# Two more feed-forward pairs as seven block products, with two weight sums of each pair added by transfers

## The chip, the core and the metric

The kernel runs on one core of a Trainium2 chip. A core has TensorE (matmul, "PE" in the profile; its loading of the stationary operand is "PEld"), VectorE ("DVE"), ScalarE ("ACT"), GpSimd ("POOL") and SyncE ("SP", which only issues transfers here), a memory of 128 partitions that all of them share, PSUM banks into which TensorE accumulates, and 16 DMA engines. Each engine works through its own instructions in the order in which the program was built, and waits for others by semaphores. The metric is the device time of one execution in microseconds, and less is better.

## The reference

One layer of a decoder trunk on 256 tokens of width 1024: RMSNorm, a convolution module beside sparse attention, an output projection, cross-attention into 256 memory tokens, and a SwiGLU feed-forward of inner width 2816, each added to the residual, then a last RMSNorm. The change touches the feed-forward alone:

```python
def swiglu(h, w_in, w_out):          # w_in (1024, 5632), w_out (2816, 1024)
    a, b = jnp.split(h @ w_in, 2, axis=-1)
    return (jax.nn.silu(a) * b) @ w_out
...
    h = rms_norm(x, norm_ffn_g[l])
    x = x + swiglu(h, ffn_in_w[l], ffn_out_w[l])
return rms_norm(x, final_norm_g)
```

Everything is float32.

## The kernel before, in words

**Numbers.** To keep float32 precision, a factor is split in two parts of TensorE's faster format: ScalarE copies it (the high part, a name that ends in h) and VectorE subtracts that from the original (the low part, l). `split` (L173 and L175) does this for a transferred tile, `part` (L284 and L285) for a computed one. A product then takes three matmuls: high by high, low by high, high by low (`three`, L1194).

**First product of the feed-forward.** The loop over 22 chunks f0 to f21 (L1162, L1164) multiplies the normalized input `fg`, which lies in the double buffer LL, with 128 gate and 128 value columns at a time. Each chunk comes in two loads of 512 KB through four buffers of tag "w", which SP fills in order as they come free. ScalarE and VectorE combine the halves, apply 1/rms (L1167), silu and the product, and `part` splits the chunk's result for the second product.

**Second product.** The 22 chunks form 11 pairs. A pair is a 256x256 left factor (2 token blocks by 2 chunks, a11 to a22) times a 256x1024 right factor (2 chunks by 2 column halves of 512, b11 to b22). Plainly that is eight block products of three 128x512 matmuls each, added into four accumulators (`four_products`). The pairs in the tuple `SEVEN` use seven block products instead, by sums of blocks: four sums of the left blocks (`factors`, L1094, VectorE and one `part` while the first product still runs), four sums of the right blocks (`side`, L1104, VectorE), and three accumulators of their own (m1, m5 to m7), which the end combines (L1229). Such a pair has 21 matmuls instead of 24.

**Where the weights come from.** A pair's right factor is two loads of 512 KB. For the first pair of `SEVEN`, pair 1, they come long before and are worked on in pieces between the chunks (`weights_ahead`). For the others `weights_of_seven` loads w0 and w1 into "w" buffers (L1110), makes the four sums in a tile `tr`, and splits three plain blocks and four sums: each other pair into the fixed tiles th and tl, the rest through the five-deep buffers of `split` (ft). Pairs outside `SEVEN` use `half` (L212). The right factors' seven parts feed `seven_products`.

**The end.** The accumulators are combined on VectorE (L1229, L1280), squared on ScalarE, multiplied with the gain `gf` (L1236, two of them on GpSimd), scaled and sent. x3 and junk, the last stage's tiles, take over the buffer LL.

**Order.** The code is traced once, and a scheduler sets the order of each engine's instructions at build time; on the chip that order is fixed. `behind` and `in_line` keep some of them behind others on their engine.

Of the kernel before, what the change touches and what calls it, by code (L numbers as in the profile page):

```python
# [96 lines left out]
def tile_hybrid_block(  # L97
# [984 lines left out]
    even_odd, sums_of, parts, shl45 = [], {}, {}, []  # L1082

    def factors(i, even, odd):

# [4 lines left out]
        raw = small(f"sr{i}", [P, 4, P], tag="vw", bufs=4)  # L1090
        a11, a21, a12, a22 = even[:, 0:P], even[:, P:S], odd[:, 0:P], odd[:, P:S]
        for to, a, b, op in ((0, a21, a22, ALU.add), (1, a11, a21, ALU.subtract), (2, raw[:, 0], a11, ALU.subtract),
                             (3, a12, raw[:, 2], ALU.subtract)):
            nc.vector.tensor_tensor(out=raw[:, to], in0=a, in1=b, op=op)  # L1094
# [3 lines left out]
    SIDES = ((0, (0, 1), (0, 0)), (1, (1, 0), (0, 1)), (2, (1, 0), 0), (3, (1, 1), 2))  # L1098

    def side(tr, w, n):  # L1100

# [2 lines left out]
        return nc.vector.tensor_tensor(out=tr[:, to], in0=pick(a), in1=pick(b), op=ALU.subtract)  # L1104

    def weights_of_seven(i):

        w0, w1 = w = [small(f"fo{i}_{n}", [P, 2, 512], tag="w", bufs=4) for n in range(2)]
        for n in range(2):
            nc.sync.dma_start(w[n], wfo[i, n])  # L1110
# [16 lines left out]
        return bs + ts

    def weights_ahead(i):

# [1 line left out]
        w = [both[:, 0:2], both[:, 2:4]]
        for n in range(2):
            nc.sync.dma_start(w[n], wfo[i, n])
# [3 lines left out]
        for n in range(4):  # L1138
            side(tr, w, n)
# [296 lines left out]
```

## Time and profile before

| | |
|---|---|
| median of 3 runs | 546.23 us (546.1 to 546.39) |
| the profiled execution's own time | 546.24 us |
| its span, first to last instruction | 544.5 us |
| granted TensorE clock, mean | 0.997 of full speed |
| first product, first and last chunk's matmuls | about 355 to 485.6 us |
| second product, to its last matmul | 464.9 (pair 1's first), then 475.9 to 538.3 us |
| busy in the span: PE, DVE, ACT, POOL | 536.9, 457.1, 356.5, 150.2 us |
| fo loads (second product's weights) | 22 of 512 KB, median 4.0 us from issue to landing |

A timeline row gives start, duration, engine, line, operation, output<-inputs, shape and, in brackets, how long the engine had been idle before and what ended it. Rows on SPq are the issue of a transfer, not the transfer. A row of a stretch table is named by its two times. Names are the program's with buffer numbers left out, so fo stands for the weights of every pair and also for the four accumulators. GpSimd issues no transfer in this kernel.

### The profile page before, as it was taken

The numbers are of one execution on the slowest core, as the hardware profiler recorded it, in microseconds if no ns is written. First come the engines' busy times: TensorE is split into PE (matmuls) and PEld (weight loads), VectorE is DVE, ScalarE is ACT, GpSimd is POOL, SyncE is SP. The second block draws the span as 40 slices with busy tenths as digits, with TensorE's granted clock in tenths as the row PEclk, the third lists the DMA queues.
The fourth block names the chain that finished last, engine by engine and source line by source line (L and its number), as shares of the span: only waits on it lengthen the run. The fifth ranks groups of instructions, "written<-read, shape, count | busy, mean of one in ns | idle before, by whom it ended". The sixth has DMA issues, their size and how long they took to land.

```text
span 544.5 us, 10498 instructions
## 1 busy us (share of the span) xinstructions
PE 536.9 (99%) x3970; PEld 502.7 (92%) x3970; DVE 457.1 (84%) x914; ACT 356.5 (65%) x642; POOL 150.2 (28%) x103
## 2 busy tenths in 40 slices
PE   9999999999999999999999999999999999999995
PEld 8999999999999998999999999988888888888874
DVE  3998999899889898975859676688899998898986
ACT  4676466678855978779447664556665676647553
POOL 0069999898990000300004000230000000000001
PEclk9999999999999999999999999999999999999998
DMA  8927955554424653334755643536455664535632
GB/s 303 406 89 260 360 162 188 198 178 155 155 99 147 205 172 114 119 117 156 227 189 173 225 156 99 175 117 222 162 183 198 194 201 154 184 126 169 217 119 78
DMA packets 29155, 97.32 MB, mean 179 GB/s; under 512 B 3120, under 2 KB 5680, under 8 KB 28848
## 3 DMA queue, kind: packets, MB, share of 16 engines
q1 hardware_dynamic: 28384, 95.42, 52.4%
q10 hardware_dynamic: 720, 1.23, 0.6%
q8 instruction: 31, 0.51, 0.4%
q14 instruction: 20, 0.16, 0.1%
HBM read 95.39 MB, written 1.25 MB: 177 GB/s over the span
## 4 chain that ended last, share of the span: by engine, by line
PE 61%; DVE 1%; issue 0%; DVEq 0%
PE ps_f L1162 15%; PE ps_f L1164 8%; PE fo L1194 7%; PE ps_pw L240 4%; PE ps_xq L240 4%; PE ps_wo L240 4%; PE ps_xo L240 4%; PE ps_v L240 4%; PE m L1194 3%; PE xo_ps L964 1%; PE xs L964 1%; PE o L795 1%; PE pt_a L774 1%; PE s L729 1%; PE o L792 1%; PE pt_b L774 0%
## 5 line engine op out<-in xcount | busy, mean ns | idle before, releaser
L416 DVE SCALAR_TENSOR_TENSOR yp<-vt,ppt,yp 128x256 f32<-128x256 f32 x196 | 78.5, 484 | 0.3
L1236 POOL TENSOR_TENSOR x<-y,gf 128x512 f32<-128x512 f32 x2 | 2.6, 1297 | 172.6 <-issue 172.6
L1162 PE MATMUL ps_f<-g,f_1h 128*128 128x512 f32 x176 | 49.1, 398 | 0.0
L1162 PE MATMUL ps_f<-g,f_0h 128*128 128x512 f32 x176 | 48.2, 396 | 0.0
L1162 PEld LDWEIGHTS ps_f<-g,f_1h 128*128 128x128 f32 x176 | 32.9, 188 | 7.5
L1162 PEld LDWEIGHTS ps_f<-g,f_0h 128*128 128x128 f32 x176 | 30.1, 188 | 4.0
L175 DVE TENSOR_TENSOR f_1l<-f,f_1h 128x1024 fp32r<-128x1024 f32 x22 | 27.5, 1249 | 5.7 <-ACT f_1h L173 4.1
L1164 PEld LDWEIGHTS ps_f<-g,f_0l 128*128 128x128 f32 x176 | 27.0, 189 | 3.9
L1164 PE MATMUL ps_f<-g,f_0l 128*128 128x256 f32 x176 | 28.3, 283 | 0.0
L175 DVE TENSOR_TENSOR f_0l<-f,f_0h 128x1024 fp32r<-128x1024 f32 x22 | 26.8, 1219 | 1.7 <-ACT f_0h L173 1.7
L173 ACT ACTIVATE f_1h<-f 128x1024 fp32r<-128x1024 f32 x22 | 23.3, 1057 | 7.5 <-PE ps_xo L240 3.7
L1164 PE MATMUL ps_f<-g,f_1l 128*128 128x256 f32 x176 | 26.5, 281 | 0.0
L175 POOL TENSOR_TENSOR u_0l<-u,u_0h 128x1024 fp32r<-128x1024 f32 x7 | 17.3, 2467 | 31.1 <-DVE kt L502 31.1
L173 ACT ACTIVATE f_0h<-f 128x1024 fp32r<-128x1024 f32 x22 | 23.1, 1050 | 1.3 <-PE ps_xo L240 1.3
L749 ACT ACTIVATE p<-p,mins 128x256 f32<-128x256 f32 x32 | 15.9, 501 | 11.7 <-DVE mins L734 11.7
L1165 ACT ACTIVATE ab<-ps_f 128x256 f32<-128x256 f32 x44 | 16.5, 375 | 10.5 <-PE ps_f L1164 10.3
L1164 PEld LDWEIGHTS ps_f<-g,f_1l 128*128 128x128 f32 x176 | 23.3, 188 | 0.0
L428 POOL TENSOR_TENSOR yt<-yt,vw 128x512 f32<-128x512 f32 x17 | 23.0, 1353 | 0.7 <-ACT vw L425 0.3
L1166 DVE TENSOR_TENSOR ab<-ps_f,ab 128x256 f32<-128x256 f32 x44 | 18.3, 419 | 3.4 <-ACT ab L1165 3.2
L1169 ACT ACTIVATE sl<-ab 128x256 f32<-128x256 f32 x22 | 9.2, 417 | 15.4 <-DVE ab L1167 14.9
L284 ACT ACTIVATE uh<-sl 128x256 fp32r<-128x256 f32 x22 | 9.1, 414 | 14.0 <-DVE sl L1170 13.9
L944 POOL COPY acc<-s_wo 128x256 f32<-128x256 f32 x1 | 0.7, 659 | 62.6 <-ACT s_wo L937 62.6
(629 smaller groups left out, 1711.9 us busy)
## 6 DMA issues: line engine op xcount, KB each, us to landing
f<-in_wst_dram SPq DMA_DIRECT2D x44, 512.0 KB, 5.7
fo<-in_wfo_dram SPq DMA_DIRECT2D x22, 512.0 KB, 4.0
u<-in_wst_dram SPq DMA_DIRECT2D x14, 512.0 KB, 7.7
q<-in_wst_dram SPq DMA_DIRECT2D x8, 512.0 KB, 5.1
ga<-in_wst_dram SPq DMA_DIRECT2D x8, 512.0 KB, 3.8
gc<-in_wst_dram SPq DMA_DIRECT2D x8, 512.0 KB, 3.8
v<-in_wst_dram SPq DMA_DIRECT2D x8, 512.0 KB, 6.6
pw<-in_wst_dram SPq DMA_DIRECT2D x8, 512.0 KB, 4.8
```

The costliest lines, as they stand in the source:

```text
L173: copy = nc.scalar.activation(hi, w, AF.Copy)
L175: splits[name] = copy, eng.tensor_tensor(out=lo, in0=w, in1=f(hi[:]), op=ALU.subtract)
L240: mm = nc.tensor.matmul(ps[:, b], lhsT=lhsT, rhs=rhs, start=row + b + kb == 0, stop=kb == NB - 1 and row == 2 and b == 1)
L416: nc.vector.scalar_tensor_tensor(out=out[:, i] if t == ts[-1] else acc[i], in0=v, scalar=w, in1=acc[i], op0=ALU.mult, op1=ALU.add)
L428: nc.gpsimd.tensor_tensor(out=yt[:, 0:2], in0=yt[:, 0:2], in1=pr, op=ALU.add)
L749: exp.append(nc.scalar.activation(p1[k][:, br], p1[k][:, br], AF.Exp, scale=-1.0, bias=mins[:, hd, 1, br:br + 1], accum_out=sums[:, hd, 1, ...
L964: mm = nc.tensor.matmul(o, lhsT=lhsT, rhs=rhs, start=n == 0, stop=n == len(order) - 1)
L1162: nc.tensor.matmul(ps, lhsT=hs[kb // 4][0][:, kb % 4, cs], rhs=fg[:, :, kb], start=kb == 0, stop=False)
L1164: nc.tensor.matmul(ps[:, 1], lhsT=hs[kb // 4][1][:, kb % 4, cs], rhs=fg[:, 0, kb], start=False, stop=kb == NB - 1)
L1165: nc.scalar.activation(ab[:, b], ps[:, 0], AF.Copy)
L1166: joins[b] = nc.vector.tensor_tensor(out=ab[:, b], in0=ps[:, 1], in1=ab[:, b], op=ALU.add)
L1194: mm = nc.tensor.matmul(o, lhsT=a[x], rhs=b[w], start=start and n == 0, stop=stop and n == 2)
```

## The change

`SEVEN` grows from pairs 1, 2, 4, 5, 7, 8 to pairs 1 to 8. Of the four sums of right blocks, two no longer run on VectorE. For these, `paired` loads two neighbouring blocks (512 KB) into a tile with a plain transfer from SP, and GpSimd then issues a second transfer of 512 KB, which reads the blocks shifted by one from HBM and adds them to the tile in place (`accum_op=ALU.add`). The host's order of the blocks and the signs of the sums are changed to suit (the sums are additions now, and some later additions are subtractions). VectorE makes the two remaining sums from these (`side`, L1116 now) in one half of a tile `spare`.

The plain blocks come in a load of 256 KB and one of 512 KB, so a pair moves 1.75 MB instead of 1 MB. The tiles for the transferred sums are: for pair 1 the tile `tr` of `weights_ahead`; for pair 2 a second half of `gf`; for pairs 3 to 6 the halves of junk and x3, which lie in LL; for pairs 7 and 8 the second half of gf and the first half of junk again. Two more sets of left sums need homes as well: spare places in uh2 and ul2, and buffers of tag p0.

```diff
-SEVEN = (1, 2, 4, 5, 7, 8)
+SEVEN = (1, 2, 3, 4, 5, 6, 7, 8)
...
+    homes, coming = [], []
+
+    def paired(i, t):
+
+        nc.sync.dma_start(t, wfo[i, :, 0:2])
+        nc.gpsimd.dma_start(t, wfo[i, :, 1:3], accum_op=ALU.add)
+        return t
+
+    def side(tb, ta, w, n):
+
+        return nc.vector.tensor_tensor(out=tb[:, n], in0=w[:, n], in1=(ta, tb)[n][:, 0], op=ALU.add)
+
+    def ahead_of(i):
+
+        n = SEVEN.index(i) - 1
+        if n == 1:
+            homes.extend(t[:, c] for t in (junk, x3) for c in range(2))
+        coming.append(paired(i, homes[n % 5]))
...
     def weights_of_seven(i):
-        w0, w1 = w = [small(f"fo{i}_{n}", [P, 2, 512], tag="w", bufs=4) for n in range(2)]
-        for n in range(2):
-            nc.sync.dma_start(w[n], wfo[i, n])
-        tr = long(f"tr{i}", 10, (P, 4, 512))
-        for n in range(4):
-            with behind(*joins[n // 2:n // 2 + 1] if i == SEVEN[1] else ()):
-                side(tr, w, n)
-        b0, b1 = split(w0[:, 0:1], [P, 1, 512], f"fo{i}_0"), split(w1, [P, 2, 512], f"fo{i}_1")
+        w0 = small(f"fo{i}_0", [P, 1, 512], tag="w", bufs=4)
+        w1 = small(f"fo{i}_1", [P, 2, 512], tag="w", bufs=4)
+        nc.sync.dma_start(w0, wfo[i, :, 0:1])
+        nc.sync.dma_start(w1, wfo[i, :, 2:4])
+        n = SEVEN.index(i)
+        ta, tb = coming[n - 1], spare[:, 2 * (n % 2):2 * (n % 2) + 2]
+        for nxt in SEVEN[len(coming) + 1:n + 3]:
+            ahead_of(nxt)
+        for k in range(2):
+            with behind(*joins[k:k + 1] if i == SEVEN[1] else ()):
+                side(tb, ta, w1, k)
+        b0, b1 = split(w0, [P, 1, 512], f"fo{i}_0"), split(w1, [P, 2, 512], f"fo{i}_1")
...
     def weights_ahead(i):
...
+        paired(i, tr[:, 0:2])
+        nc.sync.dma_start(both, wfo[i])
...
-    gf = long("gf", 11, (P, 2, 512))
-    nc.sync.dma_start(gf, gfo)
+    gf = long("gf", 11, (P, 4, 512))
+    nc.sync.dma_start(gf[:, 0:2], gfo)
+    homes.append(gf[:, 2:4])
...
+        if j == 12:
+            ahead_of(SEVEN[1])
...
+    spare = long("spare", 10, (P, 4, 512))
```

In the built programs the places that matter are these. The first is SP's queue in the second product (fo4_1 is the second load of pair 4; x3 stands for the tile that holds x3 and junk). Before:

```order
L1110 DMA fo2_0_6131<-in_wfo_dram 128x1024
L1110 DMA fo2_1_6132<-in_wfo_dram 128x1024
L212 DMA fo3_0_6177<-in_wfo_dram 128x1024
L212 DMA fo3_1_6195<-in_wfo_dram 128x1024
L1110 DMA fo4_0_6213<-in_wfo_dram 128x1024
L1110 DMA fo4_1_6214<-in_wfo_dram 128x1024
L1110 DMA fo5_0_6257<-in_wfo_dram 128x1024
```

And now:

```order
L1129 DMA fo2_0_6149<-in_wfo_dram 128x512
L1130 DMA fo2_1_6150<-in_wfo_dram 128x1024
L1129 DMA fo3_0_6196<-in_wfo_dram 128x512
L1130 DMA fo3_1_6197<-in_wfo_dram 128x1024
L1129 DMA fo4_0_6239<-in_wfo_dram 128x512
L1110 DMA x3_6085<-in_wfo_dram 128x1024 x4
L1110 DMA gf_4716<-in_wfo_dram 128x1024
L1130 DMA fo4_1_6240<-in_wfo_dram 128x1024
L1129 DMA fo5_0_6284<-in_wfo_dram 128x512
```

The plain loads of five sums stand between fo4_0 and fo4_1: pairs 3 to 6, whose home is LL, and pair 7. The first of the four waits for the last matmul on fg.

The second place is VectorE behind the last chunk (sl21 is that chunk's product; an l at the end of a name is a low part; L175 is a split, L1104 or L1116 a sum). Before:

```order
L175 TENSOR_TENSOR fo3_0l_6180<-fo3_0_6177,fo3_0h_6179 128x1024
L285 TENSOR_TENSOR ul2_4713<-sl21_6060,uh2_4710 128x256
L1104 TENSOR_TENSOR tr4_6217<-fo4_0_6213 128x512
L1104 TENSOR_TENSOR tr4_6217<-fo4_1_6214,fo4_0_6213 128x512
L175 TENSOR_TENSOR fo3_1l_6198<-fo3_1_6195,fo3_1h_6197 128x1024
L175 TENSOR_TENSOR fo4_0l_6223<-fo4_0_6213,fo4_0h_6222 128x512
L1104 TENSOR_TENSOR tr4_6217<-fo4_1_6214,tr4_6217 128x512
L175 TENSOR_TENSOR fo4_1l_6227<-fo4_1_6214,fo4_1h_6226 128x1024
```

And now:

```order
L175 TENSOR_TENSOR fo3_1l_6209<-fo3_1_6197,fo3_1h_6208 128x1024
L285 TENSOR_TENSOR ul2_4713<-sl21_6077,uh2_4710 128x256
L175 TENSOR_TENSOR fo4_0l_6248<-fo4_0_6239,fo4_0h_6247 128x512
L175 TENSOR_TENSOR fo4_1l_6252<-fo4_1_6240,fo4_1h_6251 128x1024
L1116 TENSOR_TENSOR spare_6084<-fo3_1_6197,x3_6085 128x512
L285 TENSOR_TENSOR tl3_6213<-x3_6085,th3_6212 128x1024
L1116 TENSOR_TENSOR spare_6084<-fo4_1_6240,x3_6085 128x512
L1116 TENSOR_TENSOR spare_6084<-fo3_1_6197,spare_6084 128x512
L175 TENSOR_TENSOR ft4_0l_6256<-x3_6085,ft4_0h_6255 128x1024
```

The split of fo4_1 now stands ahead of all sums of pairs 3 and 4, which need the transferred sums in x3's tile.

The third is GpSimd's queue around the sum of squares behind the cross-attention (acc_2, from which the feed-forward's 1/rms comes):

```order
L1111 DMA gf_4716<-in_wfo_dram 128x1024
L944 COPY acc_2_3990<-s2_xo0_4596 128x256
L946 TENSOR_TENSOR acc_2_3990<-acc_2_3990,s2_xo0_4596 128x256
L946 TENSOR_TENSOR acc_2_3990<-acc_2_3990,s2_xo1_4617 128x256 x2
L946 TENSOR_TENSOR acc_2_3990<-acc_2_3990,s2_xo2_4656 128x256 x2
L946 TENSOR_TENSOR acc_2_3990<-acc_2_3990,s2_xo3_4695 128x256 x2
L1111 DMA tr1_5031<-in_wfo_dram 128x1024
L1111 DMA x3_6085<-in_wfo_dram 128x1024 x4
```

The first and the last two rows are new; the adds between them stand as before. Each new row waits until the plain load into the same tile has landed.

More of the change, by code (lines that the diff above doesn't have):

```diff
@@ L1081, in tile_hybrid_block @@
     sh03, sl03 = (long(n, at, (P, 4, 4, P), F32R) for n, at in (("sh03", 0), ("sl03", 9)))
-    even_odd, sums_of, parts, shl45 = [], {}, {}, []
+    even_odd, sums_of, parts, shl = [], {}, {}, []
+    SPARE = 4
     def factors(i, even, odd):
         n = SEVEN.index(i)
-        if n == 4:
-            shl45.append(long("shl45", 14, (P, 2, 2, 4, P), F32R))
-        hi, lo = (sh03[:, n], sl03[:, n]) if n < 4 else (shl45[0][:, 0, n - 4], shl45[0][:, 1, n - 4])
+        if n == SPARE:
+            hi, lo = (t[2][:, 6:8].rearrange("p k (a b) -> p (k a) b", a=2) for t in (uh, ul))
+        elif n == SPARE + 1:
+            hi, lo = (small(f"s{c}{i}", [P, 4, P], F32R, tag="p0", bufs=2) for c in "hl")
+        elif n < SPARE:
+            hi, lo = sh03[:, n], sl03[:, n]
+        else:
+            if not shl:
+                shl.append(long("shl", 14, (P, 2, 2, 4, P), F32R))
+            hi, lo = (shl[0][:, c, n - len(SEVEN) + 2] for c in range(2))
@@ L1123, in weights_of_seven @@
             ts = []
-            for n in (0, 2):
-                both = split(tr[:, n:n + 2], [P, 2, 512], f"ft{i}_{n}")
+            for n, t in ((0, ta), (2, tb)):
+                both = split(t, [P, 2, 512], f"ft{i}_{n}")
                 ts += [[t[:, k] for t in both] for k in range(2)]
@@ L1131, in weights_ahead @@
         both = long(f"fo{i}", 14, (P, 4, 512))
[L1132 to L1134 removed]
         tr = long(f"tr{i}", 10, (P, 4, 512))
+        paired(i, tr[:, 0:2])
+        nc.sync.dma_start(both, wfo[i])
         th, tl = (long(f"t{c}{i}", at, (P, 4, 512), F32R) for c, at in (("h", 12), ("l", 13)))
         bs = []
[L1138 to L1139 removed]
+        for n in range(2):
+            side(tr[:, 2:4], tr[:, 0:2], both[:, 2:4], n)
             yield
@@ L1226, in tile_hybrid_block, with added @@
     wide = slice(0, 512)
-    def added(o, a, b):
-        nc.vector.tensor_tensor(out=o, in0=a, in1=b, op=ALU.add)
+    def added(o, a, b, op=ALU.add):
+        nc.vector.tensor_tensor(out=o, in0=a, in1=b, op=op)
         return o
@@ L1245, in tile_hybrid_block @@
             for c in range(2):
-                w = half(wfo[i, c], f"fo{i}_{c}")
+                w = half(wfo[i, :, 2 * c:2 * c + 2], f"fo{i}_{c}")
                 for tb in range(2):
@@ L1251, in tile_hybrid_block @@
     nc.scalar.activation(u1, own[1], AF.Copy)
-    u2 = added(small("more4", [P, 512], tag="nb", bufs=2), own[6], u1)
+    u2 = added(small("more4", [P, 512], tag="nb", bufs=2), own[6], u1, ALU.subtract)
     added(u25, own[5], u2)
@@ L1256, in tile_hybrid_block @@
     for i in range(early, NF // 2):
-        w = half(wfo[i, 0], f"fo{i}_0")
+        w = half(wfo[i, :, 0:2], f"fo{i}_0")
         for tb in range(2):
@@ L1296, in sent @@
         nc.sync.dma_start(out[rows, cut:], x[:, cut:])
-    ws = {i: half(wfo[i, 1], f"fo{i}_1") for i in range(early, NF // 2)}
+    ws = {i: half(wfo[i, :, 2:4], f"fo{i}_1") for i in range(early, NF // 2)}
     for i, w in ws.items():
```

25 lines of the change are left out of this document (9 added, 16 removed).

## The prediction, as put on record

> **What bounds the kernel now.** I read the page's busy times first, then a table by stretches over the feed-forward, then the timelines of TensorE and VectorE in its second product, then the transfers.
>
> ```profile
> PE 536.9 (99%) x3970; PEld 502.7 (92%) x3970; DVE 457.1 (84%) x914; ACT 356.5 (65%) x642; POOL 150.2 (28%) x103
> 400.00:440.00 40.00, 40.00 (x230) 34.99 (x229) 36.89 (x69) 26.89 (x50) 0.00 (x0) 1.00 0.55 183
> 490.00:500.00 10.00, 10.00 (x45) 8.05 (x44) 7.99 (x11) 7.51 (x10) 0.00 (x0) 1.00 0.50 163
> 500.00:510.00 10.00, 10.00 (x45) 8.09 (x44) 9.80 (x12) 6.16 (x7) 0.00 (x0) 1.00 0.59 194
> 510.00:520.00 10.00, 10.00 (x45) 8.05 (x44) 9.74 (x12) 5.14 (x6) 0.00 (x0) 1.00 0.64 219
> ```
>
> The columns of a stretch are its length, then the busy time of PE, PE's weight loads, DVE, ACT and POOL, the granted clock, the DMA share and GB/s. TensorE has no gap in the feed-forward, so a matmul taken out there is time taken out. But in the second product VectorE stands right behind it: 9.80 and 9.74 of 10 us. Whatever VectorE loses there, TensorE loses soon after.
>
> **TensorE's saving.**
>
> ```profile
> 490.57 0.39 PE L1194 MATMUL m<-fo_0h,uh 128*128 128x512 f32 x1
> 526.94 0.40 PE L1194 MATMUL m<-ft_2l,shl 128*128 128x512 f32 x1
> ```
>
> These are the first and last matmul of pairs 2 to 8, 156 matmuls apart by the order of issue: 36.37 / 156 = 0.233 us each (the 0.39 is one matmul's length in the pipeline). Pairs 3 and 6 go from 24 to 21, six fewer: **-1.40 us** if nothing makes TensorE wait.
>
> **VectorE's work.**
>
> ```profile
> 494.72 0.69 DVE L1104 TENSOR_TENSOR tr<-fo 128x512 f32<-128x512 f32 x1
> 499.39 1.22 DVE L285 TENSOR_TENSOR tl<-tr,th 128x1024 fp32r<-128x1024 f32 x1
> 500.53 0.69 DVE L175 TENSOR_TENSOR fo_0l<-fo,fo_0h 128x512 fp32r<-128x512 f32 x1
> 501.13 0.69 DVE L1104 TENSOR_TENSOR tr<-fo,tr 128x512 f32<-128x512 f32 x1
> 524.01 1.23 DVE L175 TENSOR_TENSOR ft_0l<-tr,ft_0h 128x1024 fp32r<-128x1024 f32 x1 [1.24 <-ACT ft_0h L173]
> 535.54 0.69 DVE L1280 TENSOR_TENSOR y<-fo,more 128x512 f32<-128x512 f32 x1 [0.44 <-PE fo L1194]
> ```
>
> From start to start, a 128x1024 operation takes 1.14 us (499.39 to 500.53) and a 128x512 one 0.60. A seven-product pair cost 4 sums, one 512 split and three 1024 splits: 5 x 0.60 + 3 x 1.14 = 6.42 us. With two sums left it costs 5.22; a four-product pair costs 2.28. Second product: five sevens and five fours, 43.5 us; now seven sevens and three fours, 43.4. So the transfers' additions only pay for the two new pairs. The profile in time gets worse: a seven-product pair gives TensorE 21 x 0.233 = 4.9 us of work against VectorE's 5.22, and the two fours (5.6 against 2.28) in which VectorE caught up are gone.
>
> First product: two more sets of left factors, 4 x 0.20 + 0.60 each, less two sums of pair 1:
>
> ```profile
> 448.09 0.28 DVE L1094 TENSOR_TENSOR sr<-sl 128x128 f32<-128x128 f32 x1
> 448.29 0.42 DVE L285 TENSOR_TENSOR ul<-sl,uh 128x256 fp32r<-128x256 f32 x1
> ```
>
> That is 2.8 - 1.2 = +1.6 us over some 100 us in which VectorE idles 3.1 of every 40 (first table) and TensorE never waits: hidden, 1.6 if that cover is gone. ScalarE's two more 512-wide copies lie in idle time too (26.89 of 40).
>
> **The transfers, where the loss is.** Five of the seven sums have their homes in x3's and junk's buffer, which holds the normalized input of the first product until its last matmul. SP issues four of these loads, and pair 7's into gf's half, in one batch, and by the order of issue the batch stands *ahead* of fo4_1, the second load of pair 4:
>
> ```profile
> 484.99 0.63 PE L1164 MATMUL ps_f<-g,f_1l 128*128 128x256 f32 x4
> 486.40 1.22 DVE L175 TENSOR_TENSOR ft_0l<-tr,ft_0h 128x1024 fp32r<-128x1024 f32 x1
> 487.87 0.68 DVE L1104 TENSOR_TENSOR tr<-fo,tr 128x512 f32<-128x512 f32 x1
> 52.24 0.42 SPq L461 DMA_DIRECT2D tables<-in_rel_dram  x1
> 52.71 0.43 SPq L462 DMA_DIRECT2D tables<-in_cb_dram  x1
> 489.82 0.33 SPq L1110 DMA_DIRECT2D fo<-in_wfo_dram  x1
> ```
>
> The buffer is free at 485.6 (484.99 + 0.63). Issues go out 0.47 us apart, so the four loads leave by 487.1. The gf load waits until pair 2's split has read its home (486.40 + 1.22 = 487.6), and fo4_1 until fo2_1's buffer is free (487.87 + 0.68 = 488.5; in the kernel before it left at 489.82 with nothing ahead of it). What a load costs:
>
> ```profile
> DMA to landing us min/median/max: 3.2/4.0/5.6
> 16.00:18.00 2.00, 2.00 (x20) 2.00 (x19) 1.78 (x2) 0.84 (x2) 0.00 (x0) 1.00 1.06 418
> 18.00:20.00 2.00, 2.00 (x15) 1.83 (x14) 1.73 (x3) 1.55 (x4) 0.00 (x0) 1.00 0.99 391
> 20.00:22.00 2.00, 2.00 (x19) 2.00 (x19) 2.00 (x3) 1.85 (x2) 0.00 (x0) 1.00 1.02 410
> k0w<-in_wst_dram SPq DMA_DIRECT2D x4, 256.0 KB, 6.6
> mem_t<-in_memt_dram ACTq DMA_DIRECT2D x4, 256.0 KB
> ```
>
> A full queue moves about 410 GB/s, 1.28 us for 512 KB; the least time to landing of an fo load, 3.2, leaves 1.9 fixed. Six loads in one queue from 485.9 (issue and start) need 7.7 us (6 x 0.524 = 3.15 MB): fo4_1 lands at **495.5 at the earliest**. The accumulating transfers have no row. One waits for its plain load (485.9 + 3.2 = 489.1), then POOL issues it; POOL's nearest row is a whole 128x512 operation:
>
> ```profile
> 533.44 2.55 POOL L1236 TENSOR_TENSOR x<-y,gf 128x512 f32<-128x512 f32 x2 [172.61 <-issue]
> 349.42 0.72 POOL L944 COPY acc<-s_xo 128x256 f32<-128x256 f32 x1 [49.88 <-ACT s_xo L937]
> 358.63 2.19 POOL L946 TENSOR_TENSOR acc<-acc,s_xo 128x256 f32<-128x256 f32 x2 [1.70 <-ACT s_xo L937]
> ```
>
> 1.3 us, so its data flow from 490.4, while SP's queue still has 3.15 - 4.5 x 0.41 = 1.30 MB to move. Below: they take no share of the engines, and 495.5 stands. Above: they take half for as long as SP's queue lasts: 1.30 / 0.205 = 6.3 us, 496.7 + 1.9 = **498.6**. I take the upper end: the nearest row with two queues at work is the start, where k0w's 256 KB pieces beside ACT's mem_t loads took 6.6 us, twice what 512 KB takes alone. The Trainium skill, DMA: Bandwidth & Descriptors, section "Queues, rings and completion order", says that each DMA engine goes round the queues that have work, packet by packet; by that rule half is right and the time is 550.6, where a queue served in order of issue would give 547.5; no run here shows it for POOL's queue. By its fit for GpSimd's transfers (section "Anatomy of one DMA", 2.0 us and the bytes over 436 GB/s) one would take an estimated 3.2 us alone.
>
> How long one accumulation lasts: below, a plain load's bytes (2.6 us at half rate); above, twice, as it must read its destination as well (5.1). Up to about 5 us the fourth sum of the batch lands at 490.4 + 4 x 5.1 + 1.9 = 512.7, when VectorE gets to it (499.7 + 8 x 0.60 + 7 x 1.14 = 512.5). So either end gives the same sum.
>
> **From there to the end.**
>
> ```profile
> 489.62 1.28 ACT L160 ACT_TABLE_LOAD   x1
> 500.80 1.06 ACT L173 ACTIVATE fo_1h<-fo 128x1024 fp32r<-128x1024 f32 x1 [2.32 <-DMA fo<-in_wfo_dram]
> ```
>
> ScalarE copies fo4_1 in 1.06 us, so VectorE's next row, fo4_1's split, starts at S = 498.6 + 1.1 = 499.7. VectorE has nothing else by then, for each engine takes its rows in the built order. Its work ahead: ScalarE gets to ft2_2h's copy at 488.5, then takes fo3_0h and silu (490.4), the table load (491.7), fo3_1h (492.9); VectorE's split of that, ul and fo4_0l follow, 1.14 + 0.33 + 0.60, done near 495.1. Queued behind it are all splits and sums of pairs 3 to 8. From it to the last sum ahead of y(1,0) are 23 rows of 0.60 and 21 of 1.14: 37.7 us. In the kernel before, the same stretch (494.72 to 535.54, 27 and 19 rows, 37.9 us) took 40.8: 0.44 waiting for TensorE and 2.5 waiting for ScalarE's copies, the largest 1.24 at ft_0h, whose pair 8 twin also stands behind ScalarE's read of m1. I keep the 2.5: y(1,0) at 499.7 + 37.7 + 2.5 = 539.9 against 535.54, **+4.4 us**. TensorE's 1.40 is inside: it would be done at 534.1 and waits. What follows y(1,0) is the same code. 546.24 + 4.4 = 550.6, and as the profiled run stands 0.01 above the median, **550.6**. Break-even is S = 495.3.
>
> Hidden:
>
> ```profile
> 340.91 0.33 SPq L204 DMA_DIRECT2D f<-in_wst_dram  x1
> f<-in_wst_dram SPq DMA_DIRECT2D x44, 512.0 KB, 5.7
> L1077 PE MATMUL fo<-cpt,x x16: 270/272/273, 355.4 to 367.7; 128*128 128x128 f32 x16
> 372.93 3.27 SPq L204 DMA_DIRECT2D f<-in_wst_dram  x3
> ```
>
> Gf's first accumulation stands in POOL's queue ahead of the sum of squares. Its load takes the place of the f load at 340.9, lands by 346.6, is issued again by POOL in 1.3, and POOL is due at 349.42 with 1.70 idle later: nothing; if it is late, the sum's end sets the 1/rms and TensorE. Pair 1's load waits for the residual's transposes (368.0) and holds f5's second load, which left at 372.93 anyway.
>
> **Rivals.**
> 1. *Faster.* The batch does not hold fo4_1 (landing by 494, below my floor), and VectorE's waits shrink by 1 us or more: TensorE sets the end, -1.4, 544.8. For it: VectorE's total is no larger. Against: six loads at 410 GB/s, and its work ahead of S ends near 495.1, which alone allows only -0.2. Chance 0.12.
> 2. *No change.* Accumulations take no share while SP's queue has work: S = 496.6, y(1,0) at 536.8, 547.5; with half of the 2.5 saved 546.3. Chance 0.13.
> 3. *Much slower.* An accumulation lasts over 5 us, in POOL's issue or the read of its destination; from there on each sum is late. At 6 us each, six in a row from 490.4, pair 8's lands at 528.3; behind it lie 9 x 0.60 + 8 x 1.14 = 14.5 us and 1.2 of waits: 544.0, +8.5, 554.7; at 8 us more still. For it: no row prices it. Against: POOL does nothing else. Chance 0.22.
>
> **Numbers.** The forecast has 0.53, its own range 548.5 to 553. What differs by over 0.2% (1.1 us) can be told from no change. Faster is rival 1; no change most of rival 2; the rest slower. The range 545.3 to 557 leaves out most of rival 1 and the far end of rival 3.
>
> **What would show it.** Right: TensorE idle 3 to 7 us in all between 498 and 530, first ahead of fo4_1's matmuls; fo4_1 lands near 498.6, over 8 us after its issue; VectorE idles about 4.5 us ahead of its split and then hardly. If fo4_1 lands by 496 and TensorE still waits, sums are late (rival 3). A gap before 480 would mean that the POOL queue or the extra factors weren't hidden. Wrong: TensorE without gaps to the end.

## The result, and the profile after

The changed kernel takes 553.42 us (median of 4 runs, 553.3 to 554.01) against 546.29 us of the kernel before beside it (546.1 to 546.39): a ratio of 1.0129, with a 95% interval of 1.0117 to 1.0141. That is 7.1 us slower, where the prediction had 4.4 us and a range up to 557.0. The profiled execution took 554.01 us, span 552.2, some 0.6 us above the median. Times here and below are medians; one of the six executions of early (560.23 us) fell into a slow state of the chip and is left out.

The chain of waits of the changed kernel over its end (start, length, what was waited for), and then the timeline rows of SP, TensorE and VectorE that belong to it:

```profile
489.12 12.97 DMA fo<-in_wfo_dram
502.19 1.06 ACT fo_1h L173
503.27 1.23 DVE fo_1l L175
...
534.71 8.23 PE fo L1219 x35
...
542.97 0.70 DVE y L1306
```

```profile
486.19 1.87 SPq L1110 DMA_DIRECT2D x<-in_wfo_dram  x4
503.30 0.80 PE L1219 MATMUL fo<-fo_1h,uh 128*128 128x512 f32 x1 [3.65 <-ACT fo_1h L173]
503.27 1.23 DVE L175 TENSOR_TENSOR fo_1l<-fo,fo_1h 128x1024 fp32r<-128x1024 f32 x1 [7.55 <-ACT fo_1h L173]
532.78 1.22 DVE L175 TENSOR_TENSOR ft_2l<-spare,ft_2h 128x1024 fp32r<-128x1024 f32 x1 [1.19 <-ACT ft_2h L173]
542.97 0.69 DVE L1306 TENSOR_TENSOR y<-fo,more 128x512 f32<-128x512 f32 x1 [0.23 <-PE fo L1219]
```

The chain names the place: fo4_1, issued at 489.12 behind the batch, was on its way for 12.97 us. VectorE stood for 7.55 us ahead of its split, TensorE ran dry for 3.65 us. From 503.27 on VectorE works nearly without a break to y(1,0) at 542.97, which stood at 535.54 before.

The same stretches as in the table of before (length, busy PE, weight loads, DVE, ACT, POOL, granted clock, DMA share, GB/s):

```profile
400.00:440.00 40.00, 40.00 (x230) 35.00 (x229) 37.70 (x75) 27.25 (x50) 0.00 (x0) 1.00 0.57 187
490.00:500.00 10.00, 9.65 (x42) 7.46 (x40) 4.32 (x6) 4.33 (x8) 2.60 (x3) 1.00 1.02 300
500.00:510.00 10.00, 6.70 (x18) 5.32 (x19) 6.72 (x8) 4.81 (x5) 1.71 (x2) 0.66 1.06 250
510.00:520.00 10.00, 9.78 (x43) 7.52 (x42) 9.79 (x13) 7.21 (x9) 0.88 (x1) 1.00 0.94 259
```

The first product is untouched: TensorE 40.00 of 40. From 490 to 510 the transfer engines are full (1.02 and 1.06 of their time) and yet move only 300 and 250 GB/s, where full engines moved 391 to 418 at the start of the kernel before. VectorE drops to 4.32 of 10 and then has no time left to catch up (9.79 of 10 from 510 on).

GpSimd's queue, and the row of its transfer queue on the page (packets, MB, share of 16 engines over the span). The two last rows are the time from issue to landing of the first and of the second of the batch:

```profile
q0 software_dynamic: 1152, 4.19, 4.0%
```

```profile
490.54 0.86 POOL L1111 DMA_DIRECT2D x<-in_wfo_dram  x1 [113.94 <-DMA x<-in_wfo_dram]
492.00 0.88 POOL L1111 DMA_DIRECT2D x<-in_wfo_dram  x1 [0.60 <-DMA x<-in_wfo_dram]
494.28 0.87 POOL L1111 DMA_DIRECT2D x<-in_wfo_dram  x1 [1.40 <-DMA x<-in_wfo_dram]
500.94 0.86 POOL L1111 DMA_DIRECT2D x<-in_wfo_dram  x1 [5.79 <-issue]
504.33 0.86 POOL L1111 DMA_DIRECT2D gf<-in_wfo_dram  x1 [2.53 <-issue]
```

```profile
DMA to landing us min/median/max: 10.1/10.1/10.1
...
DMA to landing us min/median/max: 12.1/12.1/12.1
```

Eight accumulations of 512 KB kept the engines for 4.0% of 552.2 us, 2.76 us each; a plain load of that size needs 1.28 at 410 GB/s. In the batch they took 10 to 13 us to land.

### The profile page after: what moved, and what is told of

It is laid out like the page before. It is cut to its first block, busy times and chain, and to the rows that moved or that the text cites. A ratio compares the mean times of both kernels' runs of the same rounds, so it can differ in the third digit from the quotient of the medians.

```text
span 552.2 us, 10534 instructions
## 1 busy us (share of the span) xinstructions
PE 539.8 (98%) x3964; PEld 503.8 (91%) x3964; DVE 458.0 (83%) x920; ACT 359.7 (65%) x648; POOL 157.3 (28%) x111
## 4 chain that ended last, share of the span: by engine, by line
PE 53%; DVE 4%; DMA 4%; ACT 1%; issue 1%; ACTq 0%; DVEq 0%
PE ps_f L1185 15%; PE ps_f L1187 7%; PE ps_pw L240 4%; PE ps_xq L240 4%; PE ps_wo L240 4%; PE ps_xo L240 4%; PE ps_v L240 4%; DMA fo<-in_wfo_dram 4%; PE fo L1219 2%; PE xo_ps L964 1%; PE xs L964 1%; DVE spare L1116 1%; PE o L795 1%; DVE fo_1l L175 1%; PE pt_a L774 1%
## 5 line engine op out<-in xcount | busy, mean ns | idle before, releaser
L1111 POOL DMA_DIRECT2D x<-in_wfo_dram x5 | 4.3, 869 | 131.1 <-DMA x<-in_wfo_dram 115.9
L175 DVE TENSOR_TENSOR f_1l<-f,f_1h 128x1024 fp32r<-128x1024 f32 x22 | 27.4, 1247 | 5.0 <-ACT f_1h L173 3.8
L175 DVE TENSOR_TENSOR f_0l<-f,f_0h 128x1024 fp32r<-128x1024 f32 x22 | 26.8, 1218 | 1.7 <-ACT f_0h L173 1.7
L175 POOL TENSOR_TENSOR u_0l<-u,u_0h 128x1024 fp32r<-128x1024 f32 x7 | 17.3, 2474 | 31.4 <-DVE kt L502 31.4
L749 ACT ACTIVATE p<-p,mins 128x256 f32<-128x256 f32 x32 | 15.9, 503 | 12.1 <-DVE mins L734 12.1
L175 DVE TENSOR_TENSOR fo_1l<-fo,fo_1h 128x1024 fp32r<-128x1024 f32 x10 | 12.2, 1221 | 9.8 <-ACT fo_1h L173 8.7
```

The lines of the kernel that those rows point to most:

```text
L175: splits[name] = copy, eng.tensor_tensor(out=lo, in0=w, in1=f(hi[:]), op=ALU.subtract)
L749: exp.append(nc.scalar.activation(p1[k][:, br], p1[k][:, br], AF.Exp, scale=-1.0, bias=mins[:, hd, 1, br:br + 1], accum_out=sums[:, hd, 1, ...
```

## Experiments

The kernel before ran beside each (546.33 to 546.45 us); the ratio to it and the 95% interval of that stand in brackets. A span of time from the first load of the batch to fo4_1's split on VectorE is the measure of how late the weights come: 17.08 us in the changed kernel (486.19 to 503.27).

### What holds fo4_1: the addition, the second queue, or the batch itself

**no_add**

```diff
-        nc.gpsimd.dma_start(t, wfo[i, :, 1:3], accum_op=ALU.add)
+        nc.gpsimd.dma_start(t, wfo[i, :, 1:3])
```

> The changed kernel with its GpSimd transfers plain: they overwrite the tile instead of adding to it, so the sums of right blocks are left out and the results of the feed-forward are not the reference's; order of work, bytes and queues are the same. Theory: in the changed kernel fo4_1 landed 13.0 us after its issue (at 502.1), because an accumulation keeps the transfer engines busy for longer than its bytes do; its queue row says 4.0% of 552 us for eight of them, 2.76 us each, against 1.28 us for a plain load of 512 KB at 410 GB/s. Then plain transfers give SP's queue half of the rate, as the prediction had it: fo4_1 lands near 498.6, VectorE starts its split near 499.7, and the time is 550.0 (553.4 less the 3.5 us by which it lands earlier), 549 to 551. Rival: it is the second queue as such, in whatever mode, that holds SP's loads; then fo4_1 lands at 501 to 503 again and the time is 553.4, 552.6 to 554.

**one_load**

```diff
-        nc.gpsimd.dma_start(t, wfo[i, :, 1:3], accum_op=ALU.add)
+        pass
```

> The changed kernel without its GpSimd transfers: the sums that they make are left out, so the feed-forward's results are not the reference's. SP's six loads stand ahead of fo4_1's landing as before, but alone. Theory: fo4_1 lands at 495.5, the floor of the prediction (3.15 MB at 410 GB/s from 485.9, and 1.9 us), its split starts near 496.6, and with the 39.7 us that the changed kernel took from there to y(1,0) this stands at 536.3, 546.8 in all, 546 to 548. Rival: VectorE's work for the two new pairs is what costs, and not the landing; then the time stays above 550.

**held** (one_load with the changed kernel's order; plain_blocks holds the loads and the splits of a pair's plain blocks, taken out of weights_of_seven)

```diff
+        if i == SEVEN[2]:
+            plain[SEVEN[3]] = plain_blocks(SEVEN[3])
...
-            with behind(*joins[k:k + 1] if i == SEVEN[1] else ()):
+            with behind(*joins[k:k + 1] if i == SEVEN[1] else splits["fo4_1"][1:] if i in SEVEN[2:4] else ()):
                 side(tb, ta, w1, k)
...
+                with behind(*splits["fo4_1"][1:] if i == SEVEN[2] else ()):
+                    part(th[:, n:n + 2], tl[:, n:n + 2], t)
```

> The changed kernel again without the GpSimd transfers (their sums left out, so the feed-forward's results are not the reference's), but with the order of the changed kernel put back: SP's queue is the same as there, and the sums of pairs 3 and 4 and pair 3's split stand behind fo4_1's split on VectorE. In the run without these transfers the scheduler had put pair 3's rows ahead of it, fo4_1's split still started at 499.4, yet the time was 544.66. Theory (the chain of the prediction): a late fo4_1 costs what stands behind it on VectorE. fo4_1 lands near 498.2, its split starts near 499.4, and the 39.4 to 39.7 us from there to y(1,0) give 538.9, that is 549.6; 548.5 to 550.6. Rival: the second transfers cost by their traffic only, and the order on VectorE does not matter: 544 to 546.

Measured: no_add 552.20 us (ratio 1.0106, 1.0091 to 1.0121), one_load 544.66 (0.9969, 0.9957 to 0.9981), held 548.91 (1.0044, 1.0031 to 1.0058). The queue row of no_add, then timeline rows of no_add, of one_load and of held (the first load of the batch, fo4_1's split, y(1,0)):

```profile
q0 software_dynamic: 1152, 4.19, 2.1%
```

```profile
485.51 1.88 SPq L1110 DMA_DIRECT2D x<-in_wfo_dram  x4
494.80 0.53 POOL L1111 DMA_DIRECT2D x<-in_wfo_dram  x1 [0.73 <-DMA x<-in_wfo_dram]
501.60 1.23 DVE L175 TENSOR_TENSOR fo_1l<-fo,fo_1h 128x1024 fp32r<-128x1024 f32 x1 [6.55 <-ACT fo_1h L173]
```

```profile
485.56 1.89 SPq L1110 DMA_DIRECT2D x<-in_wfo_dram  x4
499.40 1.23 DVE L175 TENSOR_TENSOR fo_1l<-fo,fo_1h 128x1024 fp32r<-128x1024 f32 x1 [0.48 <-ACT fo_1h L173]
533.99 0.69 DVE L1306 TENSOR_TENSOR y<-fo,more 128x512 f32<-128x512 f32 x1 [0.76 <-PE fo L1219]
```

```profile
485.41 1.88 SPq L1110 DMA_DIRECT2D x<-in_wfo_dram  x4
498.73 1.23 DVE L175 TENSOR_TENSOR fo_1l<-fo,fo_1h 128x1024 fp32r<-128x1024 f32 x1 [3.76 <-ACT fo_1h L173]
537.83 0.69 DVE L1317 TENSOR_TENSOR y<-fo,more 128x512 f32<-128x512 f32 x1 [0.60 <-PE fo L1230]
```

From the batch's first load to the split: 13.32 us in held (no second transfers), 16.09 in no_add (second transfers, plain), 17.08 in the changed kernel (second transfers that add). So the second queue costs 2.8 us and the addition as such 1.0. These are single executions, and one_load and held, with the same transfers up to fo4_1, differ by 0.5 us here; the medians of no_add and of the changed kernel lie 1.2 us apart. The theory of no_add, that the addition is the main cost, fell; the time lies 0.4 us below its rival's range. The addition does nearly double the time in the engines (4.0% against 2.1%, 2.76 against 1.44 us each), but fo4_1 feels little of it.

The trace also has a record of each packet (a row of 2 or 4 KB) with its queue, and these show how the queues share. GpSimd's first packet of the batch moved only at 494.04 in no_add and at 494.78 in the changed kernel, 4.1 and 4.2 us after GpSimd's first issue of the batch. From then on packets of both queues began in equal numbers: 321 of GpSimd's and 328 of SP's began between 494 and 500 in no_add, 243 and 241 between 495 and 502 in the changed kernel. The Trainium skill's rule of turns among queues (DMA: Bandwidth & Descriptors, section "Queues, rings and completion order") agrees with this. But a GpSimd packet of 4 KB held its engine for 182 ns in no_add and for 344 ns where it adds, against 188 ns for one of SP's. So SP's loads had 0.48 of the engines' time in no_add and 0.34 in the changed kernel in these stretches.

one_load and held have the same transfers up to fo4_1, and the split stands 13.84 and 13.32 us after the batch began; yet they lie 4.25 us apart. In one_load the scheduler had put the sums and splits of pair 3 ahead of fo4_1's split, so VectorE had work while it waited, and TensorE's saving showed: 544.66, the time that the prediction's first rival gave (544.8). In held those rows stand behind the split as in the changed kernel, and 39.1 us follow it. So one_load's expectation (546.8) fell and its rival with it, and held's (549.6, 548.5 to 550.6) came true. This shows the prediction's mechanism alone: a late load costs what the engine's order has put behind it.

### Moving the batch

**behind**

```diff
-        nc.sync.dma_start(w1, wfo[i, :, 2:4])
+        own_load = nc.sync.dma_start(w1, wfo[i, :, 2:4])
...
-            ahead_of(nxt)
+            with behind(own_load):
+                ahead_of(nxt)
```

> The changed kernel with each plain load for a later pair's sum placed behind its own pair's second load on SP's queue: three loads of the batch (pairs 3 to 5) still stand ahead of fo4_1, those of pairs 6 and 7 behind it. Theory: 1.57 MB less... that is, two loads of 512 KB fewer go ahead of fo4_1. In the changed kernel the queue moved its last 1.3 MB beside the accumulations in some 10 us; without two loads there is about 0.25 MB left when the accumulations start, so fo4_1 lands at 495 to 497 and its split starts by 498. Pair 3's sum then becomes the next thing that is late: its accumulation landed at 500.6 in the changed kernel, with less beside it perhaps 499, against 499 when VectorE gets to it: 548.5 in all, 547 to 550. Rival: accumulations take the engines from everything, so the order of SP's loads does not matter: 552.5 to 554.

**early**

```diff
+        if j == 15:
+            spare = long("spare", 10, (P, 4, 512))
+            homes += [spare[:, 0:2], spare[:, 2:4]]
+            for i in SEVEN[2:4]:
+                ahead_of(i)
...
-        ta, tb = coming[n - 1], spare[:, 2 * (n % 2):2 * (n % 2) + 2]
-        for nxt in SEVEN[len(coming) + 1:n + 3]:
-            ahead_of(nxt)
+        ta, tb = coming[n - 1], junk[:, n % 2]
+        for nxt in SEVEN[len(coming) + 1:n + 4]:
+            with behind(own_load):
+                ahead_of(nxt)
...
```

> The changed kernel with other homes for the transferred sums: pair 3's and pair 4's go into the two halves of the tile spare, which is free from about the 15th chunk on, so that they are loaded and added to during the first product; VectorE's own two sums go into junk; pairs 5 to 8 into x3, gf's half and spare again, each load behind that of an earlier pair on SP's queue. Theory: fo4_1 has two loads of 512 KB ahead of it (pairs 5 and 6) and only two accumulations beside it, so it lands by 495 and no sum is late; VectorE's total is that of the kernel before, and TensorE's saving of 1.4 us shows in part: 545.6, 544.8 to 547. Rival: the accumulations disturb the loads in the first product, or VectorE can't keep up with seven pairs of seven products in a row (5.22 us of work a pair against TensorE's 4.9, so 0.3 us more for each): 547 to 550.

Measured: behind 550.95 us (1.0103, 1.0070 to 1.0135), early 547.80 (1.0030, 1.0017 to 1.0042). Rows of behind, then of early (fo there is fo6_0, the first load of pair 6; th is the high part of pair 5's sums):

```profile
494.92 1.06 ACT L173 ACTIVATE fo_1h<-fo 128x1024 fp32r<-128x1024 f32 x1 [0.94 <-PE m L1220]
499.40 0.86 POOL L1111 DMA_DIRECT2D x<-in_wfo_dram  x1 [5.65 <-issue]
499.17 0.69 DVE L1116 TENSOR_TENSOR spare<-fo,x 128x512 f32<-128x512 f32 x1 [3.83 <-DMA x<-in_wfo_dram]
```

```profile
507.79 0.63 ACT L173 ACTIVATE fo_0h<-fo 128x512 fp32r<-128x512 f32 x1 [2.12 <-DMA fo<-in_wfo_dram]
508.33 1.04 ACT L284 ACTIVATE th<-x 128x1024 fp32r<-128x1024 f32 x1
509.42 0.50 PE L1225 MATMUL m<-th,uh 128*128 128x512 f32 x1 [2.02 <-ACT th L284]
```

In behind, fo4_1 is there by 494.92, as expected, and the wait moves on: VectorE stands 3.83 us for pair 3's sum, whose accumulation landed at 499.2. The rival said the order of SP's loads did not matter; it does, by 2.5 us between the medians (one of the four runs of behind took 554.24), but the time is 1 us above the theory's range. In early, pairs 3 and 4 were added up in time and fo4_1 was early (its split began at 495.89). But GpSimd issued the accumulations of pairs 5, 6 and 7 at 490.22, 491.25 and 499.99, and fo6_0, issued at 495.84, took 11.84 us beside them in the chain of waits. ScalarE's copy of pair 5's sums stands behind that of fo6_0, and TensorE ran dry for 2.02 us. (These rows are of an execution of 549.33 us, 1.5 above the median.) The theory of early (545.6) fell to its rival's time, for another reason than the rival gave. In both placings the accumulations of this stretch held up something that was needed next, only another thing each time.

### The two halves of the change by themselves

**vector_sums** (eight pairs, no transfers for sums)

```diff
-        nc.sync.dma_start(t, wfo[i, :, 0:2])
-        nc.gpsimd.dma_start(t, wfo[i, :, 1:3], accum_op=ALU.add)
...
+                added(ta[:, k], w0[:, k], (w0[:, 1], w1[:, 0])[k])
...
```

> Eight pairs as seven products, with all four sums on VectorE and no transfers for them: the other part of the change alone. Theory: VectorE is the bound. The two new pairs cost it 2 x (6.42 - 2.28) = 8.3 us in the second product, where it idled some 6 us between 476 and 536 in the kernel before, perhaps half of it of use, so y(1,0) comes 2.3 to 5.3 us later: 548.5 to 551.5, 549.5 taken. Rival: all of the loss comes from the transfers and VectorE has room: TensorE's saving shows, 544.8.

**six** (transfers for sums, the old six pairs)

```diff
-SEVEN = (1, 2, 3, 4, 5, 6, 7, 8)
+SEVEN = (1, 2, 4, 5, 7, 8)
```

> The six pairs of the kernel before, with the two sums of each by transfers as in the changed kernel: this part of the change alone. VectorE has 1.2 us less to do for each of five pairs, TensorE nothing less. Theory: the batch (four loads here, pairs 4, 5, 7 and 8) stands ahead of fo4_1 again; it lands 2 us earlier than in the changed kernel, near 500, and pair 3's plain products give TensorE work of its own meanwhile, but behind fo4_1's split stands VectorE's work for pairs 4 to 8: y(1,0) near 501.2 + 31.8 + 2.0 = 535, and TensorE idles 1 to 3 us ahead of pair 4: 547 to 549.5. Rival: with VectorE relieved of 6 us nothing waits: 546.2 to 546.6, and the two new pairs are what costs.

Measured: vector_sums 556.56 us (1.0181, 1.0158 to 1.0204), six 547.17 (1.0014, 1.0003 to 1.0026). Rows of vector_sums (pair 7's last sums; y(1,0)), then of six (fo4_1's split; y(1,0)):

```profile
529.48 1.23 DVE L285 TENSOR_TENSOR tl<-tr,th 128x1024 fp32r<-128x1024 f32 x1 [1.94 <-ACT th L284]
546.25 0.69 DVE L1303 TENSOR_TENSOR y<-fo,more 128x512 f32<-128x512 f32 x1 [1.25 <-PE fo L1217]
```

```profile
499.85 1.23 DVE L175 TENSOR_TENSOR fo_1l<-fo,fo_1h 128x1024 fp32r<-128x1024 f32 x1 [3.60 <-ACT fo_1h L173]
536.16 0.69 DVE L1306 TENSOR_TENSOR y<-fo,more 128x512 f32<-128x512 f32 x1 [1.31 <-PE fo L1219]
```

Two more pairs cost 10.1 us when VectorE makes all sums; the expectation had 3. It had let VectorE hide half of its 8.3 us in idle time. VectorE's idle time between 476 and 494 does fall, from 3.3 to 1.4 us, but from 494 to y(1,0) it grows from 2.2 to 6.2, above all by three waits for ScalarE's copies of sums (1.13, 1.13 and 1.94 us): y(1,0) is 10.7 us later.

The transfers alone cost 0.7 us, at the lower end of what was expected, and the trace of six shows none of it in the second product: the last matmul on ps_f begins at 485.9 against 485.3 in the kernel before, and y(1,0) is 0.6 us later too, as is the first matmul on ps_f already (355.5 against 354.9). VectorE waits 3.60 us for fo4_1 there too, but has 6 us less to do, and TensorE has pair 3's plain products meanwhile and no gap, where 1 to 3 us were expected. So of the two parts the two new pairs are the dear one, and the transfers do relieve VectorE: the changed kernel, with both, is 3.1 us faster than eight pairs without them.

### Other ways to the same sums

**pool_sums**

```diff
+        for k in range(2):
+            nc.gpsimd.tensor_tensor(out=ta[:, k], in0=w0[:, k], in1=(w0[:, 1], w1[:, 0])[k], op=ALU.add)
...
```

> Eight pairs as seven products, the two sums that the changed kernel has added by transfers made by GpSimd's own additions from the blocks as they lie in the load buffers: 1.30 us for 128x512 by its rows, 2.6 us a pair against TensorE's 4.9, in an engine that had nothing else to do; a pair moves 1 MB as before. Theory: what the run without the second transfers showed (544.66) needs no shortcut: no batch of loads stands ahead of fo4_1, VectorE has two sums a pair, TensorE sets the end: 544.7, 544.2 to 545.6. Rival: GpSimd's additions slow VectorE's rows beside them, or come late for a pair by their 2.6 us: 546.5 to 549.

**in_hbm**

```diff
+STORE_AT = (4, 7, 9, 12, 15, 18)
...
+    def store(i):
+        stored[i] = paired(i, drp.tile([P, 2, 512], F32, name=f"sums{i}")[:])
...
+            nc.sync.dma_start(homes[n % 5], stored[i])
...
+        if j in STORE_AT:
+            with behind(loads[f"f{j}_1"]):
+                store(SEVEN[2 + STORE_AT.index(j)])
```

> The changed kernel with the sums of pairs 3 to 8 added in HBM instead of in place: during the first product SP copies two neighbouring blocks into a tile in HBM and GpSimd adds the shifted blocks to it there, one pair every two or three chunks; in the second product only the finished sums are loaded into their homes, where the changed kernel had its first plain loads. The whole reference is computed. Theory: the second product then has the traffic and VectorE's order of the run that left GpSimd's transfers out, and takes its time: 544.7, 544.3 to 545.4, with TensorE without gaps, provided that TensorE does not wait in the first product either. Rival: eight transfers' additions and copies in HBM (some 4 us of all transfer engines each by 2.76 + 1.28, so 24 us over 76 us in which they were busy 0.55 of the time) hold up the weights of the first product, and TensorE waits there: 547 to 552.

**late_table**

```diff
-    with tc.issue_after(silu.ins):
-        roots("roots1")
...
+    with behind(splits["fo5_1"][0]):
+        roots("roots1")
```

> The kernel with sums in HBM, with ScalarE's table load moved from the end of the first product to behind the copy of fo5_1. Open point: in the run without GpSimd's transfers the six loads took 12.1 us instead of the prediction's 9.6, and the transfer engines moved only 238 GB/s in the two microseconds from 490 to 492, just when the table load ran (490.5 to 491.8). Theory: the table load holds back the loads; without it there those two microseconds are at 380 to 440 GB/s and fo4_1 lands some 0.8 us sooner after the first load of the batch. Rival: the dip stays at the same place, the table load has nothing to do with it. The time is that of the run beside it either way, within 0.5 us.

**hbm_sooner**

```diff
-STORE_AT = (4, 7, 9, 12, 15, 18)
+STORE_AT = ("pw1_1", "pw2_1", "pw3_1", "wo1_0", "f9_1", "f12_1")
...
+    for k in STORE_AT[:4]:
+        with behind(loads[k]):
+            store(SEVEN[2 + STORE_AT.index(k)])
...
```

> The kernel with sums in HBM again, with its additions moved to where the transfer engines had less to do: pairs 3 to 6 between the loads of the conv projection and of the first output projection (about 225 to 260 us, where the kernel before shows them busy 0.33 to 0.44 of the time and GpSimd idle from 223 to 286), pairs 7 and 8 at chunks 9 and 12. In the run with all of them in the first product TensorE waited 1.0 us once, at 387, for a weight that came late there, and had no gap from then on. Theory: that gap is the whole difference to the run without GpSimd's transfers; without it 544.7 to 545.3, faster than the kernel before. Rival: the time lost lies in the second product or in later loads, and moving the additions changes nothing: 546.2 to 547.2.

Measured: pool_sums 555.23 us (1.0156, 1.0133 to 1.0179), in_hbm 546.74 (1.0019, 1.0006 to 1.0031), late_table 547.90 (1.0027, 1.0009 to 1.0045), hbm_sooner 545.18 (0.9981, 0.9970 to 0.9991).

Groups of pool_sums by line and shape between 490 and 530 for VectorE, 484 and 530 for GpSimd (count, busy, mean ns of one):

```profile
L175 DVE TENSOR_TENSOR fo_1l<-fo,fo_1h 128x1024 fp32r<-128x1024 f32 x6 | 9.5, 1577 | 0.0
...
L1134 POOL TENSOR_TENSOR x<-fo 128x512 f32<-128x512 f32 x5 | 10.5, 2098 | 9.3 <-PE ps_f L1187 6.7 <-DMA fo<-in_wfo_dram 2.5
```

The expectation of pool_sums (544.7) fell, and far beyond its rival. GpSimd's additions are no free work. A 128x512 addition took 2.10 us instead of 1.30, and VectorE's 128x1024 split 1.58 on average instead of 1.22: the two engines hold each other up, and VectorE, busy for 30.00 of the 30 us from 500 to 530, is the bound here. VectorE's 128x1024 splits take either 1.21 us or about 2.31, and each of the long ones between 470 and 530 overlaps a GpSimd addition. The Trainium skill names this contention (SBUF — State Buffer, section "Who interferes with whom": a VectorE operation with two inputs in SBUF contends with a GpSimd operation that reads SBUF); these rows agree.

Rows of in_hbm: TensorE's only gap from 340 us on, the stretch around it, and two microseconds of the batch with ScalarE's table load beside them; then the same two microseconds of the batch in held, whose five sums' loads read from the weights themselves:

```profile
387.27 1.20 PE L1196 MATMUL ps_f<-g,f_1h 128*128 128x512 f32 x4 [1.01 <-ACT f_1h L174]
380.00:400.00 20.00, 18.99 (x107) 16.21 (x106) 16.96 (x32) 12.76 (x23) 0.86 (x1) 1.00 0.97 279
491.82 1.28 ACT L161 ACT_TABLE_LOAD   x1
491.00:492.00 1.00, 1.00 (x6) 0.83 (x5) 1.00 (x2) 0.98 (x3) 0.00 (x0) 1.00 1.02 389
492.00:493.00 1.00, 1.00 (x6) 0.77 (x6) 1.00 (x3) 1.00 (x1) 0.00 (x0) 1.00 0.99 397
```

```profile
490.00:491.00 1.00, 1.00 (x6) 0.81 (x5) 1.00 (x2) 0.98 (x2) 0.00 (x0) 1.00 0.91 238
491.00:492.00 1.00, 1.00 (x6) 0.78 (x5) 0.67 (x2) 0.99 (x3) 0.00 (x0) 1.00 0.80 217
486.00:497.60 11.60, 11.60 (x52) 9.35 (x51) 7.24 (x11) 6.11 (x9) 0.00 (x0) 1.00 0.93 327
```

late_table was to show that the table load causes the dip to 238 and 217 GB/s. It could not, as the kernel that it was built on has no dip: in_hbm has the table load at 491.8 and 389 to 397 GB/s. That alone shows that the table load is not enough to cause it. What differs between the two is where the five loads read from (whole blocks in HBM there, 4 KB of every 8 KB of the weights here); that this is the cause was not tested. The time of late_table lies 1.2 us above in_hbm's, more than the 0.5 expected, in intervals that overlap; its second product is not slower (48.7 us from the last matmul on ps_f to y(1,0), as in in_hbm).

The time of in_hbm (546.74, twelve runs from 546.15 to 549.86; the profiled one is the fastest) lies between its theory's 544.7 and its rival's 547 to 552. The rival had the mechanism: additions in the first product held up one weight load, at 387 where the transfer engines were busy 0.97 of the time. The second product went as the theory said: from the last matmul on ps_f (486.6) to y(1,0) (535.34) it takes 48.7 us, as in one_load (485.3 to 533.99). hbm_sooner issues four of the six additions between 232 and 266, where the engines had been busy 0.33 to 0.66 of the time, and is the version that beats both kernels, with the whole computation; its time is in the range of its theory. Its rows (GpSimd's first addition, fo4_1's copy, a stretch of the second product, y(1,0)):

```profile
231.98 1.01 POOL L1112 DMA_DIRECT2D sums<-in_wfo_dram  x1 [8.10 <-DMA sums<-in_wfo_dram]
496.33 1.06 ACT L174 ACTIVATE fo_1h<-fo 128x1024 fp32r<-128x1024 f32 x1 [0.20 <-PE fo L1236]
500.00:510.00 10.00, 10.00 (x44) 8.08 (x44) 10.00 (x13) 7.22 (x9) 0.00 (x0) 1.00 0.48 172
534.49 0.69 DVE L1323 TENSOR_TENSOR y<-fo,more 128x512 f32<-128x512 f32 x1 [1.25 <-PE fo L1236]
```

TensorE has no gap in the feed-forward, VectorE waits for TensorE at the end, and y(1,0) stands at 534.49, 1.05 earlier than in the kernel before. Counted from the last matmul on ps_f (485.8 against 485.3) it comes 1.5 us earlier, all of the 1.40 that the two pairs save.

## Why the prediction was right, and what in it was not

**Direction, place and mechanism: right.** The batch ahead of fo4_1, VectorE stopping at fo4_1's split, TensorE idle first ahead of fo4_1's matmuls (3.65 us; 4.2 in all between 498 and 530, within the 3 to 7 forecast), no gap before 480, and everything behind the split pushed back: each is in the profile as told, and held shows it without the second transfers. The sizes were too small: fo4_1 was to land near 498.6 and landed at 502.1, VectorE was to idle about 4.5 us ahead of its split and idled 7.55, and 553.42 us lies just outside the forecast's own range (548.5 to 553). All three go back to the landing below.

**The chain from the split to y(1,0): right to 0.5 us.** 40.2 us were forecast (37.7 of work and 2.5 of waits), 39.70 measured. The largest wait, 1.19 us, fell on pair 8, as the prediction had it, though on its second split of sums and not on the first.

**The landing of fo4_1: this is the term that was mis-sized.** S was to be 499.7 and was 503.27, 3.6 us later. Against the prediction's steps:

| step, from the batch's first load to fo4_1's split | predicted | measured | from |
|---|---|---|---|
| six loads in one queue, with the copy | 10.7 (485.9 to 496.6) | 13.32 | held |
| more by a second queue that takes half | 3.1 | 2.77 | no_add less held |
| more by the addition | 0 | 0.99 | after less no_add |
| sum | 13.8 | 17.08 | after |

The rest of the 3.6 is that the batch began at 486.19, not at 485.9; this execution is 0.5 us late at the start of the first product already (355.4 against 354.9).

The first step failed because the prediction took its earliest possible landing, 495.5, for the landing itself. It counted six loads at 410 GB/s in order of issue. In held the engines moved 327 GB/s over the 11.60 us until fo4_1 landed (the last row of held's stretches above), 3.79 MB, though the six loads are 3.15 MB: 0.64 MB belong to loads issued behind fo4_1 (the first packets of fo5_0, told by their 2 KB, moved at 495.5). Whether these took engines from fo4_1, or moved between its last packet and its landing, was not separated. They are 1.6 us at 410 GB/s; the two microseconds at 238 and 217 GB/s are another 0.9. Together with the 7.7 and 1.9 of the prediction they give 12.1 of the 12.2 us measured from 485.41 to 497.6.

The second step came out nearly right, in part by luck. The prediction had the second queue's data flow from 490.4, with 1.30 MB of SP's loads left, at half of the rate. In the changed kernel the data flowed from 494.78, with 0.84 MB left, and SP's queue moved 126 GB/s between 495 and 502 instead of 205: a later start and a smaller share offset each other. Nor did the row from which the half was taken show it: on the same page the u loads of 512 KB, in one queue, took 7.7 us, longer than k0w's 6.6. What shows the even turns are the packets of no_add.

**"Either end gives the same sum": wrong by 1 us, by a path that was left out.** How long an accumulation lasts was tied to the lateness of sums alone. That is where it did nothing (no wait of VectorE in the changed kernel ended on an accumulation, though they took 10 to 13 us to land), since VectorE itself was late. But its time in the engines also comes out of SP's loads: as many packets of each queue, and each that adds takes 1.9 times as long.

**Rivals.** The first (fo4_1 lands by 494, 544.8) did not happen. Its time came in one_load by another way: fo4_1 lands only near 498 there, but VectorE has work ahead of the split, and that gave 544.66. The second (accumulations take no share: 547.5) is 1.4 us below held's 548.91, the run in which they take none, because its landing was too early: S = 496.6 against 498.73. The third (sums late) did not happen in the changed kernel but is what behind turned into.

**VectorE's total** was forecast to be unchanged, 43.5 to 43.4 us, and the page agrees (457.1 us busy before, 458.0 after, with 1.6 us more in the first product by the prediction's estimate). What the prediction under-weighed is how little this total says: the two new pairs alone cost 10.1 us, so the change leans on every sum that the transfers make.

## What to carry to other kernels

Work that is moved to transfers must be priced in the time of the transfer engines and in every load that queues beside it, not only in when its own result is due; here the addition nearly doubled that time, and the second queue moved as many packets as the first. Look at what the built order puts behind a wait: the same late load cost 4.2 us more when the rows that could have run during it stood behind it. And if an engine or a queue is full in one stage, do the work in a stage where it is idle, even at the price of a second pass through HBM.
